# Output projection of three of four token blocks by Strassen's scheme on float32 head sums, and another order of VectorE's work in the first pair of each ConvFFN half

## The chip, the cores and the metric

One NeuronCore of a Trainium2 chip runs the whole kernel. The metric is the device time of one execution in microseconds (us), lower is better. TensorE (PE in the profile) multiplies matrices, VectorE (DVE), ScalarE (ACT) and GpSimd (POOL) work on elements, and SyncE (SP) issues most DMA transfers, in the order of its program.

## The reference

One decoder layer on x of 2048 tokens x 1024, in float32:

```python
h = rms_norm(x, norm_mix_pre)
p = h @ w_in                        # 1024 x 3088: u, v_a, q, k, v_b, g_out, lr
out_a = sgu_mixer(gelu(u), gelu(v_a), ...)       # causal gating in chunks of 128, 4 heads
out_b = rms_norm(gla_mixer(q, k, v_b, gk), ...) * silu(g_out)   # gated linear attention, 4 heads
mix = concatenate([out_a, out_b]) @ w_out        # 1024 x 1024
x = x + rms_norm(mix, norm_mix_post)
h = rms_norm(x, norm_ffn_pre)
up = causal_dwconv(h @ w_up, conv_w, conv_b)     # 1024 x 5632
ff = (gelu(up[..., :2816]) * up[..., 2816:]) @ w_down
x = x + rms_norm(ff, norm_ffn_post)
```

## The kernel before

**Products.** A float32 product is made of three matmuls on float32r operands. ScalarE copies an operand to its rounded high part, and VectorE or GpSimd subtracts that from the operand to get the low part ("split"). The matmuls are high x high, high x low and low x high.

**Mix phase.** Four blocks b0 to b3 of 512 tokens. Each block runs its in-projection, then two things interleaved by `weave`: "main", the linear attention (`gla_half`, matmuls named lv, o, s), and "side", a list of steps. The side of block b is: the rest of the projections g1 and g, the *output projection of block b-1* (`mix_out`), the residual of that block (`x1_steps`: read the mix rows x0m, x1m, ... and the rows of x, write x1), then `va`, `u` and the spatial gating. In block 3 the side also loads x1 rows (`h_load`), transposes and combines them for the ConvFFN (`h_combos`, tiles h0x, h1b, h01s, ...) and stores the seven sums of Strassen's scheme (`act`). Blocks overlap: block 2's first loads (b2xT0 to 3, x transposed) are issued during block 1's last steps.

**Weights.** `weight` gives a piece of two 128 x 512 tiles. At its first use a piece is read raw, copied, split (by GpSimd and VectorE in turn), and both parts are written to DRAM under a key; later blocks read the two parts. The pool has three slots for the parts and two for raw pieces, so the piece three places on can only be read when TensorE has used this one. In `mix_out` a piece (`mx0w0`, ...) serves 24 matmuls: four token tiles, two k-tiles, three matmuls. There are eight pieces, 192 matmuls in a block. Four 128 x 1024 buffers with the tag `xin` hold b2xT, the rows of x1_steps and the tiles of h_load and h_combos.

**Order.** The instruction order of the mix phase comes from a scheduler that works through the code by priority; each engine and each queue then keeps its order. The mix rows are written from ScalarE's queue.

**ConvFFN.** Two halves of 22 pairs, by Strassen's scheme with seven products (`product(m)`) of 12 matmuls each. Beside the products of one pair (`u10` is half 1, pair 0) VectorE adds partial results from PSUM (u2, u3, c22), makes the four sums of the next pair's weights (`sums`, `last_sum`), and does the convolution and the gate of the previous pair; GpSimd splits. In the first pair of a half it also splits operands of the half's activations (`acts`, tiles tal and tbl). Then follows the down projection (d0A, ...).

Of the kernel before, what the change touches and what calls it, by code (L numbers as in the profile page):

```python
# [7 lines left out]
F32 = mybir.dt.float32  # L8
# [9 lines left out]
P = 128  # L18
D = 1024
# [18 lines left out]
def layer_kernel(ctx, tc, x, xT, w_ch, w_gl, w_tk, w_o, w_up, w_dn, w_gk, wsT, cols, conv, rows, sgub,  # L38
# [14 lines left out]
    def scratch(shape, name):  # L53
# [5 lines left out]
    ffs_d = [[[scratch([P, n, T], f"ffs{h}{m}{q}") for q, n in enumerate(GROUPS)] for m in range(7)]  # L59
             for h in range(2)]  # L60
    wdn_d = [[scratch([P, n, T], f"wdn{m}{q}") for q, n in enumerate(GROUPS)] for m in range(7)]

# [58 lines left out]

    def token_steps(srcs, kper, n, hh, hl, name, done, key=None):
        nk = kper * len(srcs)
        ps = [bank(f"{name}a{t}", acc=True) for t in range(TT)]
        for i, src in enumerate(srcs):
            hi, lo = weight(src, kper * n, f"{name}w{i}", key and (key, i))
# [30 lines left out]
    def mix_phase(mp, late):  # L157
# [57 lines left out]
        def mix_in(b, prev):  # L215
# [119 lines left out]

            oh = [late.tile([P, T], F32R, tag="ohi", name=f"{n}oh{h}", bufs=4) for h in range(NH)]
            ol = [late.tile([P, T], F32R, tag="olo", name=f"{n}ol{h}", bufs=4) for h in range(NH)]
            ohb = late.tile([P, NH, T], F32R, tag="ohb", name=f"{n}ohb", bufs=1)
            olb = late.tile([P, NH, T], F32R, tag="olb", name=f"{n}olb", bufs=1)

# [4 lines left out]

            def side():
                def gate(t, ps):
# [3 lines left out]
                yield from token_steps([w_tk[0, i] for i in range(4)], 2, 512, hh, hl, f"{n}g", gate, "g")  # L351
                def g4(nm):
                    return w1.tile([P, D], F32, tag="xin", name=nm, bufs=4)

                if prev is not None:
                    for k, ins in enumerate(mix_out(b - 1, *prev)):
                        if b == 3 and k % 2 == 0:
                            xs = h_load(0, k // 2, g4)
                        yield
                        if b == 3 and k % 2:  # L360
                            with tc.issue_after(ins):
                                h_combos(0, k // 2, xs, g4, g4,
                                         lambda nm: [bank(f"{nm}{k}") for k in range(2)])
                            yield
                    if b < 3:
                        yield from x1_steps(b - 1, gpost, lambda nm: w1.tile([P, D], F32, tag="xin", name=nm, bufs=4))

                va = [w1.tile([P, 512], F32, tag="va", name=f"{n}va{t}", bufs=4) for t in range(TT)]
# [13 lines left out]
                for h in range(NH):  # L382
# [7 lines left out]
                    for t in range(TT):  # L390
# [7 lines left out]
                                           op0=ALU.mult, op1=ALU.add)  # L398
                    V.tensor_tensor(out=z, in0=z, in1=u, op=ALU.mult)
                    A.copy(out=oh[h], in_=z)  # L400
                    split_lo(V, ol[h], z, oh[h])
                    yield
# [10 lines left out]

            weave(main(), side(), (0.8, 0.8) if prev is not None else (0.62, 0.5))
            return oh + [ohb[:, h, :] for h in range(NH)], ol + [olb[:, h, :] for h in range(NH)]

        def mix_out(b, oh, ol):
            n = f"b{b}"
            for half in range(2):
                def evac(t, ps):  # L420
                    m = late.tile([P, 512], F32, tag="mo", name=f"{n}mo{t}", bufs=2)
                    A.copy(out=m, in_=ps)
                    A.activation(out=ps, in_=ps, func=AF.Square, accum_out=ssm[:, b, half, t:t + 1])
                    nc.scalar.dma_start(out=mix_d[b][t * P:(t + 1) * P, half * 512:(half + 1) * 512],
                                        in_=m)
# [11 lines left out]
    def gla_half(b, hb, cum, qT, kT, vb, sg, ohb, olb, state, attn, klow, qup, lvl_sb, sel_sb, w1, pend):  # L437
# [221 lines left out]
    def ffn_phase(fp, mix_rest, late):  # L659
# [266 lines left out]

        def rest_of(f):
            V.tensor_tensor(out=f.g[:, T:], in0=f.g[:, T:], in1=f.u2, op=ALU.add)
            f.conv_first("g")
            f.conv_rest("v")  # L930
            f.keep_halo("v")

        raws = load_up(1)
        for at, (half, j) in enumerate(steps + [(2, 0)]):
# [6 lines left out]
            turn = half == 0 and j == NPAIR - 1  # L941
            new = half == 1 and j == 0
            if at + 1 < len(steps):
                s23, s14 = unit("s", f"{n}s23", 2), unit("s", f"{n}s14", 2)
# [21 lines left out]
            if prev:  # L966
                rest_of(prev)
            if not end:
                f.u2 = w2.tile([P, T], F32, tag="u2", name=f"{n}u2")
                u3 = w2.tile([P, T], F32, tag="u3", name=f"{n}u3")  # L970
                copy_u2 = A.copy(out=f.u2, in_=pa)
            if new:
                op_split(acts[1])
            if nxt:
                nxt.sums()
                nxt.split(0)
            if new:
                op_split(acts[3], G)
            if prev:
# [8 lines left out]
            if prev:  # L988
                prev.conv_rest("g")
                A.activation(out=prev.y, in_=prev.y, func=AF.Gelu_apprx_tanh)  # L990
            product(6, None if end else pc, apart=() if end else (add_u2,))
            if new:
                op_split(acts[2])
            if not end:
                add_u3 = V.tensor_tensor(out=u3, in0=pc, in1=f.u2, op=ALU.add)
            side.turn(0)
            if nxt:
                nxt.last_sum()
                nxt.split(4)
            if prev:  # L1000
                V.tensor_tensor(out=prev.y, in0=prev.y, in1=prev.yv, op=ALU.mult)
                ff.append(prev.y)
# [3 lines left out]
            if nxt:  # L1006
                nxt.split(1)
            if len(ff) == 2:
                ph, pj = steps[at - 1]
                q, i = divmod(pj // 2, 4)  # L1010
                for m, src in stage_sums(f"f{ph}{pj}", *ff):
                    nc.sync.dma_start(out=ffs_d[ph][m][q][:, i, :], in_=src)
                ff = []
            side.sums()
            product(1, None if end else pa, True, () if end else (add_c22,))
            if nxt:
                nxt.split(3)
            if at == 0:
                op_split(acts[2])
            side.turn(1)  # L1020
# [9 lines left out]
            if not end:  # L1030
                V.tensor_tensor(out=pc, in0=pc, in1=f.u2, op=ALU.add)
                f.conv_first("v")
            side.late_sums()
            if turn:
# [120 lines left out]
        for s, (m, half, g) in enumerate(dsteps):  # L1155
# [5 lines left out]
            if s <= last:  # L1161
# [5 lines left out]
                if half == 1 and s + 3 < len(dsteps):  # L1167
                    d_load_w(dsteps[s + 3][0], g)
            if s + 1 < len(dsteps):
                op_split(dt[s + 1])  # L1170
# [109 lines left out]
```

## Time and profile before

| | |
|---|---|
| median of 3 runs | 2161.97 us (2161.17 to 2163.98) |
| profiled execution | 2162.19 us, span 2160.4 us |
| TensorE / VectorE busy | 2081.2 us (96%) / 1456.4 us (67%) |
| ScalarE / GpSimd busy | 885.4 us (41%) / 628.3 us (29%) |
| moved by DMA | 411.46 MB, mean 190 GB/s |

The span is the profiled execution from its first to its last instruction. The shares are means over stages that differ: the mix phase ends at about 842 us, half 0 of the ConvFFN at 1274, half 1 at 1733.

### The profile page before, as it was taken

Reading aid. Unit: us, or ns where it says so; the run is one execution under the profiler, and the core shown is the slowest. Engines: PE = TensorE matmul, PEld = TensorE weight load, DVE = VectorE, ACT = ScalarE, POOL = GpSimd, SP = SyncE. Lnnn points to the kernel's source line nnn. Section 1 sums busy time; section 2 is a strip of 40 time slices with the busy share of each in tenths; the row PEclk is TensorE's granted clock in tenths of the full one; section 3 lists DMA queues with packets and bytes.
Section 4 is the critical chain, followed back from the end, with each engine's and each line's share of the span. In section 5 each row is a group of like instructions: output and inputs, shape, how many; then the busy total and the mean of one; then the engine's idle time right before and its main releaser. Section 6 shows DMA issues by size and latency. Waiting matters only on the chain.

```text
span 2160.4 us, 27160 instructions
## 1 busy us (share of the span) xinstructions
PE 2081.2 (96%) x9904; PEld 1718.5 (80%) x9904; DVE 1456.4 (67%) x2010; ACT 885.4 (41%) x1462; POOL 628.3 (29%) x449
## 2 busy tenths in 40 slices
PE   7999999999999998999999988999999999999998
PEld 6888888887887776888888866887778778888886
DVE  5875646544564434888788789999999952443467
ACT  5444434333345424444555453433333333323252
POOL 2320311111110021555554555555555300000000
PEclk9999999999999999999999998999999999999999
DMA  7884567456656757455355453444444544444467
GB/s 268 284 307 176 168 245 274 156 175 238 232 172 216 257 182 276 150 185 190 108 185 181 132 209 132 161 152 146 150 156 171 196 149 138 145 160 147 142 243 263
DMA packets 160390, 411.46 MB, mean 190 GB/s; under 512 B 15344, under 2 KB 44416, under 8 KB 160256
## 3 DMA queue, kind: packets, MB, share of 16 engines
q1 hardware_dynamic: 155360, 401.22, 54.1%
q10 hardware_dynamic: 4896, 8.50, 1.0%
q8 instruction: 78, 1.28, 0.2%
q14 instruction: 56, 0.46, 0.1%
HBM read 288.42 MB, written 129.89 MB: 194 GB/s over the span
## 4 chain that ended last, share of the span: by engine, by line
PE 42%; DVE 14%; issue 3%; DMA 1%; ACT 1%; DVEq 0%; SPq 0%; POOLq 0%; POOL 0%; ACTq 0%
PE d0D L1119 3%; PE d1C L1119 3%; PE d0C L1119 3%; PE d1A L1119 3%; PE d1D L1119 2%; PE d0A L1119 2%; PE d1B L1119 1%; PE d0B L1119 1%; DMA dw<-in_w_dn 1%; DVE dw L611 1%; DVE ds L612 1%; DVE dw L613 1%; PE u017G L756 1%; PE u015G L756 1%; PE u013G L756 1%
## 5 line engine op out<-in xcount | busy, mean ns | idle before, releaser
L1099 POOL TENSOR_TENSOR o01r<-o01r,mhalf 128x4 f32<-128x4 f32 x1 | 1.0, 1007 | 357.2 <-DVE o01r L1098 357.2
L77 DVE TENSOR_TENSOR tal<-tal,tah 128x1024 fp32r<-128x1024 f32 x14 | 19.8, 1422 | 25.4 <-ACT tah L689 25.4
L494 DVE COPY_PREDICATED attn<-lvl_sb,b3h1lv 128x512 f32<-128x512 uint8 x7 | 6.3, 895 | 26.2 <-PE b3h1lv L491 26.2
L474 POOL TENSOR_TENSOR qup<-b1q,b1h0e 64x256 f32<-64x256 f32 x7 | 9.8, 1406 | 41.9 <-issue 25.1
L689 ACT CAST tah<-tal 128x1024 fp32r<-128x1024 f32 x14 | 14.5, 1047 | 17.2 <-DMA tal<-act 17.2
L474 POOL TENSOR_TENSOR qup<-b2q,b2h0e 64x256 f32<-64x256 f32 x7 | 9.8, 1407 | 40.1 <-issue 23.3
L1119 PE MATMUL d0A<-d0wh,d00th 128*128 128x512 f32 x44 | 17.9, 406 | 2.8 <-DVE u121y L783 2.8
L77 DVE TENSOR_TENSOR d05tl<-d05tl,d05th 128x1024 fp32r<-128x1024 f32 (+1 forms) x6 | 6.6, 1134 | 20.5 <-ACT d05th L689 20.5
L474 POOL TENSOR_TENSOR qup<-b3q,b3h0e 64x256 f32<-64x256 f32 x7 | 8.1, 1156 | 42.0 <-issue 23.4
L77 DVE TENSOR_TENSOR d01tl<-d01tl,d01th 128x1024 fp32r<-128x1024 f32 (+1 forms) x6 | 6.6, 1134 | 20.0 <-ACT d01th L689 20.0
L77 DVE TENSOR_TENSOR d11tl<-d11tl,d11th 128x1024 fp32r<-128x1024 f32 (+1 forms) x6 | 6.5, 1133 | 19.7 <-ACT d11th L689 19.7
L1075 DVE TENSOR_TENSOR r<-d0C,du 128x512 f32<-128x512 f32 x8 | 5.2, 686 | 21.3 <-PE d0C L1119 21.3
L77 DVE TENSOR_TENSOR tbl<-tbl,tbh 128x1024 fp32r<-128x1024 f32 x10 | 13.1, 1353 | 9.3 <-ACT tbh L689 9.3
L1119 PE MATMUL d0A<-d0wl,d00th 128*128 128x512 f32 x44 | 17.8, 404 | 1.2 <-DVE d0wl L77 1.2
L474 POOL TENSOR_TENSOR qup<-b2q,b2h1e 64x256 f32<-64x256 f32 x7 | 5.6, 804 | 44.7 <-PE b2h1lv L491 26.9
L613 DVE TENSOR_TENSOR dw<-dw,ds 128x512 f32<-128x512 f32 x11 | 17.4, 1580 | 0.4
L1119 PE MATMUL d0A<-d0wh,d00tl 128*128 128x512 f32 x44 | 17.6, 400 | 0.0
L611 DVE TENSOR_TENSOR dw<-dw 128x512 f32<-128x512 f32 x11 | 17.4, 1578 | 0.4
L612 DVE TENSOR_TENSOR ds<-dw,dw 128x512 f32<-128x512 f32 x11 | 17.4, 1578 | 0.4
L474 POOL TENSOR_TENSOR qup<-b3q,b3h1e 64x256 f32<-64x256 f32 x7 | 5.7, 817 | 40.7 <-PE b3h1lv L491 35.3
L1119 PE MATMUL d1A<-d0wh,d10th 128*128 128x512 f32 x44 | 17.1, 389 | 0.0
L1119 PE MATMUL d1A<-d0wl,d10th 128*128 128x512 f32 x44 | 17.1, 389 | 0.0
(4495 smaller groups left out, 8168.9 us busy)
## 6 DMA issues: line engine op xcount, KB each, us to landing
dw<-in_w_dn SPq DMA_DIRECT2D x22, 512.0 KB, 5.1
tal<-act SPq DMA_DIRECT2D x14, 512.0 KB, 7.6
tbl<-act SPq DMA_DIRECT2D x14, 512.0 KB, 5.8
wdn<-in_w_dn SPq DMA_DIRECT2D x6, 1024.0 KB, 9.2
out<-r SPq DMA_DIRECT2D x12, 512.0 KB, 8.0
wdn<-dw SPq DMA_DIRECT2D x22, 256.0 KB, 2.4
wdn<-ds SPq DMA_DIRECT2D x22, 256.0 KB, 3.2
d00tl<-ffs SPq DMA_DIRECT2D x5, 512.0 KB, 8.4
```

What stands on the lines that cost most here:

```text
L77: eng.tensor_tensor(out=lo, in0=full, in1=hi.bitcast(F32), op=ALU.subtract)
L474: (G if par else V).tensor_tensor(out=qu[r, :, par, :].rearrange("p a (g s) -> p a g s", s=s), in0=view(q)[r, :, :, 1, :], in1=ev[r, :, :, ...
L494: V.copy_predicated(out=av[:, :, :, 1, :], mask=mk.unsqueeze(1).to_broadcast([P, 8, gc, s]), data=ps.rearrange("p (x g s) -> p x g s", x=8 ...
L611: eng.tensor_tensor(out=b12, in0=b12, in1=b11, op=ALU.subtract)
L612: eng.tensor_tensor(out=t2, in0=b22, in1=b12, op=ALU.subtract)
L613: eng.tensor_tensor(out=t4, in0=b21, in1=t2, op=ALU.subtract)
L689: A.copy(out=hi[:, sl], in_=raw[:, sl])
L756: ins = PE.matmul(ps, lhsT=a[:, sl], rhs=b[:, i], start=not more and i == 0 and k == 0, stop=i == 3 and k == 2, skip_group_check=more)
L1075: return V.tensor_tensor(out=row(half, o[0], t)[:, o[1] * T:(o[1] + 1) * T], in0=ps, in1=u, op=ALU.add)
L1099: G.tensor_tensor(out=rs, in0=rs, in1=mhalf[:, :4], op=ALU.pow)
L1119: ins = PE.matmul(ps, lhsT=lhs, rhs=wop[w][:, i], start=start and k == 0, stop=stop and k == 2, skip_group_check=more)
```

## The change

**The projection.** For blocks 0 to 2 `mix_out_sums` takes the place of `mix_out`. The heads' outputs are kept in float32 (`ar`, `br`), not split. Seven products of Strassen's scheme follow, in the order 0, 1, 5, 6, 3, 4, 2, each on a sum of heads (`operand`) and a sum of weights, with 24 matmuls: 168 in place of 192. There are 14 weight pieces (`mx00`, `mx01`, `mx10`, ...) with 12 matmuls each. s1, s2 and s4 take buffers of the tag xin. The mix rows are written from SP's queue.

**The weight sums.** At the end of block 0's side `mix_sums` reads w_o in 16 loads of 256 KB, makes four sums in each of four steps on VectorE, and writes them in 16 stores.

**Block 3.** Its side calls h_load and h_combos at fixed steps (k = 1, 3, 5, 12, 14, 16). Its own projection stays `mix_out`; in the second half two of its four pieces have no kept parts (their keys are None), since no block before has used them alone.

**First pairs** (`fresh`). VectorE adds PSUM sums first, then the previous pair's convolution, then the weight sums. One operand of half 1 (`acts[3]`) is split by VectorE in place of GpSimd.

```diff
+        def mix_sums(g4):
+            for kt in range(4):
...
+                r1, r2, t = g4(f"ws{kt}a"), g4(f"ws{kt}b"), g4(f"ws{kt}t")
+                for k in range(2):
+                    for r, at in ((r1, i), (r2, 2 + i)):
+                        nc.sync.dma_start(out=r[:, k * T:(k + 1) * T], in_=w_o[k, at][:, sl])
+                ts = combos(V, r1[:, :T], r1[:, T:], r2[:, :T], r2[:, T:], t[:, :T], t[:, T:], r2[:, :T])
+                for m in range(3, 7):
+                    nc.sync.dma_start(out=wmx_d[m][:, kt * T:(kt + 1) * T], in_=ts[m])
+                yield
+
+        def mix_out_sums(b, ar, br, g4):
...
+            s1, s2, s4 = [g4(f"{n}s{k}").rearrange("p (k t) -> p k t", k=NH) for k in (1, 2, 4)]
+            V.tensor_tensor(out=s1, in0=a21, in1=a22, op=ALU.add)
+            V.tensor_tensor(out=a21, in0=a11, in1=a21, op=ALU.subtract)
+            V.tensor_tensor(out=s2, in0=s1, in1=a11, op=ALU.subtract)
+            V.tensor_tensor(out=s4, in0=a12, in1=s2, op=ALU.subtract)
+            src = {0: a11, 1: a12, 2: s4, 3: a22, 4: s1, 5: s2, 6: a21}
+
+            def operand(m):
+                hi, lo = [late.tile([P, NH, H], F32R, tag=f"r{k}", name=f"{n}m{m}{k}", bufs=2) for k in ("hi", "lo")]
+                A.copy(out=hi, in_=src[m])
+                split_lo(V, lo, src[m], hi)
+                return hi, lo
+
+            def keep(t, r, half, x, spare):
+                tt = r * 2 + t
+                A.activation(out=spare, in_=x, func=AF.Square, accum_out=ssm[:, b, half, tt:tt + 1])
+                nc.sync.dma_start(out=mix_d[b][tt * P:(tt + 1) * P, half * T:(half + 1) * T], in_=x)
...
+            for at, m in enumerate(DORDER):
...
+                for i in range(2):
+                    piece = wmx_d[m][:, i * D:(i + 1) * D] if m > 2 else w_o[m // 2, 2 * (m > 0) + i]
+                    wh, wl = weight(piece, D, f"{n}mx{m}{i}", ("mx", m, i))
...
+                keys = [("mx", 0, 0), ("mx", 0, 1), ("mx", 1, 0), ("mx", 1, 1)] if half == 0 else \
+                    [None, None, ("mx", 2, 0), ("mx", 2, 1)]
```

```diff
             if nxt:
-                nxt.sums()
+                if not fresh:
+                    nxt.sums()
                 nxt.split(0)
-            if new:
-                op_split(acts[3], G)
...
                 add_c22 = V.tensor_tensor(out=pb, in0=pd, in1=u3, op=ALU.add)
-            if nxt:
+            if new:
+                op_split(acts[3])
+            if fresh:
+                nxt.sums()
+                nxt.split(5)
+                nxt.split(6)
+                if prev:
+                    conv_g(prev)
+            elif nxt:
                 nxt.split(1)
```

SP's queue in block 1, behind the output projection of block 0. The names: x0m, x1m, x2m, x3m read mix rows, x0x to x3x rows of x, x10 to x13 are the x1 rows written; h and l before 1vaw, 1u, 2g0w and 2qk are the high and low parts of weights. Before, around the first b2xT:

```order
L597 DMA x2x_2961<-in_x 128x1024
L91 DMA hb1u0_3160<-kb0u00_1387 128x1024
L91 DMA lb1u0_3161<-kb0u01_1388 128x1024
L602 DMA x12_71<-x2x_2961 128x1024
L91 DMA hb1u1_3202<-kb0u10_1462 128x1024
L91 DMA lb1u1_3203<-kb0u11_1463 128x1024
L595 DMA x3m_2980<-mix0_85 128x1024
L597 DMA x3x_2982<-in_x 128x1024
L91 DMA hb1u2_3244<-kb0u20_1544 128x1024
L91 DMA lb1u2_3245<-kb0u21_1545 128x1024
L222 DMA b2xT0_3334<-in_xT 128x1024
```

And with the change:

```order
L705 DMA x2x_3061<-in_x 128x1024
L703 DMA x3m_3093<-mix0_85 128x1024
L92 DMA hb2g0w1_3539<-kb1g0w10_1825 128x1056
L92 DMA lb2g0w1_3540<-kb1g0w11_1826 128x1056
L710 DMA x12_71<-x2x_3061 128x1024
L92 DMA hb2qk0_3594<-kb0qk00_412 128x1024
L92 DMA lb2qk0_3595<-kb0qk01_413 128x1024
L705 DMA x3x_3095<-in_x 128x1024
L225 DMA b2xT0_3437<-in_xT 128x1024
L225 DMA b2xT1_3448<-in_xT 128x1024
```

The first read of block 2's input has moved from behind the third `u` piece to behind the first `qk` piece of block 2, and the residual's chain with it.

SP's queue with the change in block 3, where block 2 is projected and the second group of h rows is stored (act, from the tiles h1b, h1x, h5x and h01s of h_combos; mx50 is the first weight piece of product 5):

```order
L92 DMA hb2mx50_6035<-kb0mx500_2611 128x1024
L92 DMA lb2mx50_6036<-kb0mx501_2612 128x1024
L753 DMA act04_93<-h1x_5717 512x1x128
L753 DMA act05_94<-h5x_5720 512x1x128
L92 DMA hb2mx51_6051<-kb0mx510_2633 128x1024
L92 DMA lb2mx51_6052<-kb0mx511_2634 128x1024
L92 DMA hb2mx60_6093<-kb0mx600_2681 128x1024
L92 DMA lb2mx60_6094<-kb0mx601_2682 128x1024
L753 DMA act03_92<-h01s_5852 512x1x128
L753 DMA act06_95<-h5x_5720 512x1x128
```

The last store out of h5x, whose buffer is used again for s2, now stands behind three weight pieces of the projection.

VectorE in the first pair of half 1 before (u10s14 and u10s23 are weight sums of the next pair, u10u2 and u10u3 the additions from PSUM, tbl the low parts of the half's activations):

```order
L77 TENSOR_TENSOR tbl1_10679<-tbl1_10679,tbh1_10678 128x1024 x2
L708 TENSOR_TENSOR u10s14_10742<-u1rv_10556 128x512
L709 TENSOR_TENSOR u10s23_10741<-u1rg_10555,u1rv_10556 128x512
L710 TENSOR_TENSOR u10s23_10741<-u10s14_10742,u1rg_10555 128x512
L984 TENSOR_TENSOR u10u2_10767<-u10V_10748,u10u2_10767 128x512
L780 SCALAR_TENSOR_TENSOR u021y_10762<-u021G_10559,cv_6762,u021y_10762 128x1023
L780 SCALAR_TENSOR_TENSOR u021y_10762<-u021G_10559,cv_6762,u021y_10762 128x1022
L77 TENSOR_TENSOR tbl2_10738<-tbl2_10738,tbh2_10737 128x1024 x2
L995 TENSOR_TENSOR u10u3_10768<-u10V_10748,u10u2_10767 128x512
```

And with the change:

```order
L1109 TENSOR_TENSOR u10u2_10933<-u10V_10917,u10u2_10933 128x512
L1117 TENSOR_TENSOR u10u3_10934<-u10V_10917,u10u2_10933 128x512
L78 TENSOR_TENSOR tbl1_10848<-tbl1_10848,tbh1_10847 128x1024 x2
L888 SCALAR_TENSOR_TENSOR u021yv_10884<-u021V_10729,cv_6927,u021yv_10884 128x1023
L888 SCALAR_TENSOR_TENSOR u021yv_10884<-u021V_10729,cv_6927,u021yv_10884 128x1022
L1129 TENSOR_TENSOR u10V_10917<-u10G_10916,u10u3_10934 128x512
L78 TENSOR_TENSOR tbl3_10876<-tbl3_10876,tbh3_10875 128x1024 x2
L816 TENSOR_TENSOR u10s14_10911<-u1rv_10725 128x512
L817 TENSOR_TENSOR u10s23_10910<-u1rg_10724,u1rv_10725 128x512
L818 TENSOR_TENSOR u10s23_10910<-u10s14_10911,u1rg_10724 128x512
```

Both additions now stand ahead of the weight sums and of two splits, and the split of tbl3 is new on this engine.

## Rows read from the trace of the kernel before

**Rows 1.** The page: its head, and part 1, busy time of each engine.

```profile
span 2160.4 us, 27160 instructions
PE 2081.2 (96%) x9904; PEld 1718.5 (80%) x9904; DVE 1456.4 (67%) x2010; ACT 885.4 (41%) x1462; POOL 628.3 (29%) x449
```

**Rows 2.** Stretches of the span; the first line names the columns.

```profile
core 0: us, PE busy (x) PEld busy (x) DVE busy (x) ACT busy (x) POOL busy (x), PEclk, DMA share, GB/s
100.00:150.00 50.00, 48.80 (x267) 41.05 (x267) 36.19 (x74) 22.16 (x34) 15.01 (x13) 1.00 0.93 319
150.00:200.00 50.00, 48.93 (x287) 41.56 (x286) 31.30 (x62) 22.20 (x45) 5.44 (x4) 1.00 0.62 219
...
1330.00:1700.00 370.00, 364.80 (x1584) 295.74 (x1583) 355.82 (x415) 144.09 (x206) 199.23 (x130) 1.00 0.45 154
...
257.00:312.40 55.40, 55.19 (x284) 45.47 (x282) 22.90 (x50) 25.42 (x54) 12.84 (x10) 1.00 0.67 236
455.00:509.90 54.90, 54.90 (x283) 45.48 (x282) 17.20 (x47) 16.89 (x46) 5.57 (x7) 1.00 0.53 183
```

**Rows 3.** TensorE's timeline near 308 and 370: start, duration, instruction.

```profile
307.65 0.39 PE L135 MATMUL b0mx1a<-hb0mx1w,b0olb 128*128 128x512 f32 x1
...
310.43 0.39 PE L135 MATMUL b0mx1a<-hb0mx1w,b0olb 128*128 128x512 f32 x1
...
369.60 0.39 PE L120 MATMUL b1u<-b1hi,lb1u 128*128 128x512 f32 x1
...
370.63 0.37 PE L133 MATMUL b2g0a<-hb2g0w,b2hi 128*128 128x264 f32 x1
```

**Rows 4.** DMA from 255 to 372 in 40 slices; issues, KB, median us to landing.

```profile
GB/s 259 275 129 382 153 232 179 144 410 300 403 351 95 277 78 280 6 244 297 189 391 413 115 307 231 297 385 286 304 332 394 346 214 304 338 250 309 185 185 133
...
rb0mx1w<-in_w_o SPq DMA_DIRECT2D x4, 512.0 KB, 4.8
...
lb1vaw<-kb0vaw SPq DMA_DIRECT2D x4, 512.0 KB, 5.0
...
b2xT<-in_xT SPq DMA_DIRECT2D x4, 512.0 KB, 6.5
```

**Rows 5.** SP's queue from 300 to 352: start, issue time, transfer.

```profile
310.25 0.32 SPq L595 DMA_DIRECT2D x0m<-mix  x1
...
344.66 0.38 SPq L222 DMA_DIRECT2D b2xT<-in_xT  x1
```

**Rows 6.** Groups by line, 255 to 313: busy, mean ns; idle time before.

```profile
L95 ACT CAST hb0mx1w<-rb0mx1w 128x1024 fp32r<-128x1024 f32 x4 | 4.2, 1049 | 6.6 <-PE b0mx0a L135 6.6
...
L77 DVE TENSOR_TENSOR lb0mx1w<-rb0mx1w,hb0mx1w 128x1024 fp32r<-128x1024 f32 x2 | 2.5, 1230 | 6.3 <-ACT hb0mx1w L95 6.3
...
L77 POOL TENSOR_TENSOR lb0mx1w<-rb0mx1w,hb0mx1w 128x1024 fp32r<-128x1024 f32 x2 | 4.8, 2398 | 12.1 <-DMA mix<-b0mo 10.2 <-ACT hb0mx1w L95 1.9
```

**Rows 7.** DMA issues from 685 to 706, columns as in rows 4.

```profile
act<-h5x SPq DMA_DIRECT2D x2, 256.0 KB, 4.7
```

**Rows 8.** TensorE's waits in the whole span: total, times, longest, in us.

```profile
PE u10V L756 <- DVE u10u L995: 13.8, 1, 13.8
...
PE b3mx0a L133 <- DMA hb3mx0w<-kb0mx0w: 3.8, 1, 3.8
...
PE u00V L756 <- DVE u00u L995: 2.2, 1, 2.2
```

**Rows 9.** Stretches behind two waits of TensorE, columns as in rows 2.

```profile
200.59:204.00 3.41, 3.41 (x9) 2.65 (x9) 0.60 (x1) 3.38 (x3) 0.00 (x0) 0.50 0.00 0
...
791.10:797.90 6.80, 5.89 (x15) 4.11 (x14) 0.00 (x0) 0.62 (x1) 0.41 (x1) 0.50 0.92 370
```

**Rows 10.** VectorE's timeline in the first pair of half 1.

```profile
1290.20 2.82 DVE L709 TENSOR_TENSOR u10s<-u1rg,u1rv 128x512 f32<-128x512 f32 x1
...
1300.99 2.36 DVE L77 TENSOR_TENSOR tbl<-tbl,tbh 128x1024 fp32r<-128x1024 f32 x2 [2.12 <-ACT tbh L689]
...
1308.86 0.68 DVE L796 TENSOR_TENSOR f021b<-u020y 128x512 f32<-128x512 f32 x1
```

More of the change, by code (lines that the diff above doesn't have):

```diff
@@ L60, in layer_kernel @@
              for h in range(2)]
+    wmx_d = {m: scratch([P, 4 * T], f"wmx{m}") for m in range(3, 7)}
     wdn_d = [[scratch([P, n, T], f"wdn{m}{q}") for q, n in enumerate(GROUPS)] for m in range(7)]
@@ L120, in chan_mm, with token_steps @@
             PE.matmul(ps, lhsT=lo[:, sl], rhs=hh[kt], start=False, stop=(kt == KT - 1))
-    def token_steps(srcs, kper, n, hh, hl, name, done, key=None):
+    def token_steps(srcs, kper, n, hh, hl, name, done, keys=None):
+        if isinstance(keys, str):
+            keys = [(keys, i) for i in range(len(srcs))]
         nk = kper * len(srcs)
@@ L344, in mix_in, with g4, steps @@
                 sgu_consts()
-            def side():
+            def g4(nm):
+                return w1.tile([P, D], F32, tag="xin", name=nm, bufs=4)
+            def steps():
                 def gate(t, ps):
@@ L351, in side @@
                 yield from token_steps([w_tk[0, i] for i in range(4)], 2, 512, hh, hl, f"{n}g", gate, "g")
-                def g4(nm):
-                    return w1.tile([P, D], F32, tag="xin", name=nm, bufs=4)
                 if prev is not None:
[L356 to L364, printed above, removed]
+                    yield from mix_out_sums(b - 1, *prev, g4)
                     if b < 3:
-                        yield from x1_steps(b - 1, gpost, lambda nm: w1.tile([P, D], F32, tag="xin", name=nm, bufs=4))
+                        yield from x1_steps(b - 1, gpost, g4)
                 va = [w1.tile([P, 512], F32, tag="va", name=f"{n}va{t}", bufs=4) for t in range(TT)]
@@ L398, in side @@
                                            op0=ALU.mult, op1=ALU.add)
-                    V.tensor_tensor(out=z, in0=z, in1=u, op=ALU.mult)
-                    A.copy(out=oh[h], in_=z)
-                    split_lo(V, ol[h], z, oh[h])
+                    if whole:
+                        V.tensor_tensor(out=z, in0=z, in1=u, op=ALU.mult)
+                        if h % 2 == 0:
+                            o2, l2 = [late.tile([P, 2, T], F32R, tag=f"r{k}", name=f"{n}o{k}{h}", bufs=2)
+                                      for k in ("hi", "lo")]
+                        oh.append(o2[:, h % 2])
+                        ol.append(l2[:, h % 2])
+                        A.copy(out=oh[h], in_=z)
+                        split_lo(V, ol[h], z, oh[h])
+                    else:
+                        V.tensor_tensor(out=ar[:, h], in0=z, in1=u, op=ALU.mult)
+                    yield
+                if b == 0:
+                    yield from mix_sums(g4)
+            def side():
+                if b < NB - 1:
+                    yield from steps()
+                    return
+                xs = None
+                for k, _ in enumerate(steps()):
+                    if k in (3, 5, 14, 16):
+                        with tc.issue_after(newest_pe()):
+                            h_combos(0, (3, 5, 14, 16).index(k), xs, g4, g4,
+                                     lambda nm: [bank(f"{nm}{i}") for i in range(2)])
+                    if k in (1, 3, 12, 14):
+                        xs = h_load(0, (1, 3, 12, 14).index(k), g4)
                     yield
@@ L942, in ffn_phase @@
             new = half == 1 and j == 0
+            fresh = new or at == 0
             if at + 1 < len(steps):
@@ L1005, in ffn_phase @@
                 add_c22 = V.tensor_tensor(out=pb, in0=pd, in1=u3, op=ALU.add)
-            if nxt:
-                nxt.split(1)
[L1008 to L1013, printed above, removed]
+            if new:
+                op_split(acts[3])
[4 more added lines that the diff above has]
+                if prev:
+                    conv_g(prev)
+            elif nxt:
+                nxt.split(1)
+            if end:
+                op_split(dt[1])
+                op_split(dw[DORDER[0], 1])
+            if len(ff) == 2 and not fresh:
+                stage()
             side.sums()
             product(1, None if end else pa, True, () if end else (add_c22,))
+            if fresh:
+                op_split(acts[2])
+                nxt.last_sum()
+                nxt.split(4)
+                nxt.split(1)
+                if prev:
+                    close_y(prev)
             if nxt:
                 nxt.split(3)
-            if at == 0:
-                op_split(acts[2])
             side.turn(1)
```

107 lines of the change are left out of this document (87 added, 20 removed).

## The prediction

> **What bounds the kernel now.** I read the page first, then stretches of it, then single waits. TensorE is busy 2081.2 of 2160.4 us [rows 1], so whatever ends sooner must first make TensorE's list shorter or its waits fewer. But the page is an average, and two stretches are bound otherwise. In half 1 of the ConvFFN, VectorE is busy 355.82 of 370 us beside TensorE's 364.80: both at once [rows 2]. And in the mix phase the transfers are near what they ever reach: the highest 50 us, at 100 to 150, move 319 GB/s with the DMA engines busy for 0.93 of the time [rows 2]. The reader should keep these two in mind, since the change takes matmuls from the mix phase and adds transfers to it.
>
> The projection of block 0 is bound by TensorE before: from its first matmul to the first of `b1va` 55.40 us pass, 55.19 of them busy [rows 2]. Matmuls of 128x512 follow each other every 0.2315 us: twelve take from 307.65 to 310.43 [rows 3].
>
> **The change part by part.**
>
> *Fewer matmuls.* Seven products of 24 matmuls in place of 192: 24 less per block, 72 in all, times 0.2315 = **-16.7 us**. This is what can be gained in the mix phase, and the form of the matmul (128x512) does not change.
>
> *Block 0's own projection (in block 1).* Here each weight piece is used for the first time: it is read raw (524 KB), and its high and low parts are written out to be kept (1049 KB), so 1.573 MB per piece. Before, eight pieces come at 24 matmuls each; now fourteen at 12 each. In bytes: 14 x 1.573 = 22.0 MB and 2.1 MB of mix rows, against 12.6 + 2.1. TensorE needs 55.4 - 24 x 0.2315 = 49.8 us, with GLA's matmuls that lie between. About 1.6 MB (three raw pieces) is read ahead, and the kept parts of the last three pieces (3.1 MB) follow after, so 19.4 MB must pass in 49.8 us: 390 GB/s. The nearest row with the same traffic is 100 to 150, at 319 GB/s: 60.8 us, **+11**. Bounds: 0, since single slices of 2.9 us reach 413 GB/s [rows 4]; +16, since with two raw buffers a piece needs its landing of 4.8 us [rows 4], a copy of 1.05 and a split of 1.23 or 2.40 (VectorE and GpSimd in turn, mean 1.8) [rows 6], so 7.65 / 2 = 3.8 us against TensorE's 49.8 / 14 = 3.56: +4 from that alone, and both limits can hit different pieces.
>
> By the Trainium skill ("DMA: Bandwidth & Descriptors", Specifications) the fabric's ceiling is 435 GB/s. By it 19.4 MB would take an estimated 45 us and this term would be 0; the slice of 413 speaks for that, no row of 50 us does.
>
> *What comes behind the projection on SP's queue.* The order shows x0m, x1m, ... (the reads of the mix rows for the residual) moved behind `va` and `u` weights. Before, x0m is issued at 310.25, ahead of block 1's `va`, and the first b2xT at 344.66, right behind the third `u` piece [rows 5]. Now hb2qk0 stands ahead of b2xT0. It is the third piece after u3, and the weight pool has three slots, so it is issued only when TensorE has used u3. Before, the last matmul on u3 starts at 369.60 and b2g0a at 370.63 [rows 3]: b2xT had landed long ago. Now it is issued at about 370.0 plus four issues of 0.35, lands 6.5 later [rows 4], and ScalarE and VectorE make the operand in about 1.2 more (half of a copy and a split of twice the size [rows 6]): 379.1 against 370.63, **+8.5**. Bounds +5 (a landing of 3) and +14 (x3x, which stands ahead too, waits for its slot first). At the next block the same chain has its kept weights and a shorter queue: **+1** (0 to +6).
>
> *Head sums.* In blocks 0 to 2 the operands are made as seven copies and splits of 1.05 and 1.23 [rows 6]; VectorE has 49.8 us for 7 x 1.23, four sums and eight additions of about 0.7, about 20 us in all, beside 22.9 us of its own [rows 2]: hidden, save in block 3. There s1, s2, s4 take the slots (tag xin) that h_combos leaves. s2 gets that of h5x, whose last store (act06) stands on SP behind hb2mx60 and lb2mx60. These are the seventh piece, issued when the fourth is used, which is the end of the second product; the third product needs s2. So TensorE waits: four issues (about 2), the store's landing 4.7 [rows 7], the sum (1.23), the copy 1.05 and part of the split [rows 6]; 9 less what the order of banks gives back: **+8.5** (bounds 0, if the slots fall otherwise, and +11).
>
> *Weight sums in block 0.* 16 loads and 16 writes of 256 KB (8.4 MB) and 16 sums of 128x512. Half of it falls into 100 to 150, the fullest stretch: 4.2 MB less the 1.2 MB that a share of 0.93 leaves free, at 343 GB/s = 9 us at most; the other half falls into the next 50 us, at a share of 0.62 [rows 2]. **+6** (0 to +12).
>
> *Block 3's own projection* now has two of its pieces raw. 4.8 + 1.05 + 2.4 = 8.3 us is less than the 11.1 us of two pieces ahead, but TensorE waits there already, 3.8 for the first kept piece [rows 8]: **+2** (0 to +8).
>
> *First pairs.* In half 0 TensorE waits 2.2 for an addition that stands behind weight sums [rows 8]; it now stands ahead: **-2** (0 to -4). In half 1 it waits 13.8 for the same addition [rows 8], which now comes before the sums. But all of half 1 is bound by VectorE too [rows 2], so what counts is when VectorE is done: a sum takes 2.82 there, while GpSimd splits, and 0.68 elsewhere [rows 10]; two or three of them give about -5.4; the split that VectorE takes over costs 2.36 [rows 10]; a wait of 2.12 for ScalarE may shrink: **-4** (0 to -8).
>
> *Clock.* After a wait of some us TensorE runs at 0.50 for 3.4 us, or twice that (6.8 us after the wait at b3mx0a) [rows 9]: the granted clock is then 1.2 GHz, and half of that time is lost. Four or five new waits (block 0's pieces, b2g0a, block 3) cost 4 x 1.7: **+7** (+3 to +10).
>
> Sum: -16.7 + 11 + 8.5 + 1 + 8.5 + 6 + 2 - 2 - 4 + 7 = **+21.3**. The profiled execution took 2162.19 us, 0.2 above the median of 2161.97, so the forecast is **2183** (its own range 2173 to 2196).
>
> **The rivals.**
> 1. *Everything added is hidden* (faster). The transfers keep 390 GB/s or more in block 0, and the slots in block 3 fall well: 2162 - 16.7 - 2 - 4 + about 2 = 2141. It decides at one weight piece of 1.573 MB per 3.56 us. For it: slices of 413 GB/s. Against it: no 50 us above 319, and the two waits on SP's order (8.5 each) need no bandwidth to occur. With one of them it is 2150. Chance 0.12.
> 2. *The projection of block 0 keeps pace, the two waits remain.* 2183 - 11 - 3 (two stretches of half clock) = 2169; with the weight sums hidden too, 2163, no change. The rate of 435 would do this. Chance 0.22 in all, 0.07 of it within 0.2%.
> 3. *The kept loads stall as well.* In blocks 1 and 2 a piece is 1.049 MB per 3.56 us, 295 GB/s, and 337 with the mix rows; before, this stretch has 183 GB/s [rows 2]. By 319 the three slots just cover it. If not, up to +8 in each: 2199. Against it: a kept part lands in 5.0 us [rows 4], with two pieces (7.1 us) ahead. Chance 0.16.
>
> **How the numbers follow.** The forecast has 0.50. A measurement can tell 0.2% here, 4.3 us. Faster is rival 1: 0.12; same 0.07; slower the rest, 0.81. The range reaches from the middle between rivals 1 and 2, 2156, to 2204, where rival 3 ends with its clock.
>
> **What would show it.** In block 1, TensorE's waits on the weights named mx, the stretch of the projection longer than 55.4 us although it has 24 matmuls less, and a DMA share above 0.9. At b2g0a, a wait of about 8 on b2hi. In block 3, a wait ahead of the third product on b2m5. In half 1 the wait of 13.8 gone, but the start of the second pair earlier by 4 only. The forecast is wrong if pieces land in step with 3.56 us, or if SP's order does not hold x3m and b2xT back.

## The result

With the change the kernel takes **2203.08 us** (median of 6 runs, 2200.44 to 2205.24), before 2162.7 beside it: ratio 1.0187, 95% interval [1.0174, 1.0199]. It is 40 us slower. The forecast was 2183 in a range of 2156 to 2204: the right sign, but half the size. The range holds the result with 0.9 us to spare.

The page of the kernel with the change, its head and part 1, against [rows 1]:

```profile
span 2203.1 us, 27206 instructions
PE 2082.6 (95%) x9832; PEld 1718.1 (78%) x9832; DVE 1519.0 (69%) x2071; ACT 900.5 (41%) x1467; POOL 634.1 (29%) x451
```

TensorE has 72 matmuls less and is busy 1.4 us *longer*. That is the first thing to explain. The mix phase as one stretch shows it, first before, then after (columns as in rows 2; one fence for each kernel):

```profile
0.00:842.10 842.10, 802.68 (x4308) 671.54 (x4308) 461.31 (x902) 347.58 (x654) 153.35 (x133) 0.99 0.66 227
```

```profile
0.00:887.60 887.60, 800.60 (x4236) 670.43 (x4236) 523.72 (x961) 363.29 (x659) 164.34 (x137) 0.96 0.72 248
...
100.00:150.00 50.00, 47.46 (x264) 39.97 (x262) 35.24 (x72) 23.05 (x37) 16.07 (x14) 1.00 0.88 311
150.00:200.00 50.00, 46.34 (x256) 40.52 (x255) 32.78 (x58) 19.83 (x38) 4.87 (x3) 0.90 0.86 293
...
268.50:337.90 69.40, 56.95 (x259) 45.11 (x258) 39.77 (x68) 34.32 (x63) 22.83 (x13) 0.88 0.83 292
495.80:551.70 55.90, 54.84 (x300) 45.23 (x299) 32.42 (x67) 18.77 (x41) 7.26 (x7) 1.00 0.85 296
```

From 842.1 to 887.6 the mix phase grew by 45.5 us. The matmuls left out are worth 16.7, but busy time fell by only 2.1: the other 14.6 went into matmuls at the lower clock (mean 0.96, before 0.99). By the traces' record of the clock there are twelve stretches at 0.50 up to u00V with the change, and five before. TensorE's (PE) busy time in them, summed, with the change and then before:

```profile
sum 78.51, PE 56.16 PEld 48.17 DVE 44.82 ACT 28.72 POOL 14.11; mean PE 4.68 PEld 4.01 DVE 3.73 ACT 2.39 POOL 1.18
```

```profile
sum 23.89, PE 20.82 PEld 16.42 DVE 7.49 ACT 15.02 POOL 0.44; mean PE 4.16 PEld 3.28 DVE 1.50 ACT 3.00 POOL 0.09
```

At 0.50 up to half of that busy time is lost: 28.1 and 10.4, a difference of 17.7, which covers the 14.6. Idle time of TensorE rose from 39.4 to 87.0, by 47.6. So 47.6 + 14.6 - 16.7 = 45.5. The projection of block 0 takes 69.4 us, before 55.4 [rows 2].

TensorE's waits name the places, against [rows 8]; those of 3.9 and more:

```profile
PE b0mp L496 <- POOL lb0mx L78: 12.3, 4, 4.6
PE b2mp L494 <- ACT b2m5hi L467: 10.6, 1, 10.6
PE b2g0a L136 <- ACT b2hi L230: 8.9, 1, 8.9
PE b0g0a L136 <- ACT hb0g0w L96: 6.5, 1, 6.5
PE b3mx1a L137 <- POOL lb3mx1w L78: 4.5, 1, 4.5
PE b3mx0a L137 <- DMA lb3mx0w<-kb0mx: 3.9, 1, 3.9
PE b3mx0a L136 <- DMA hb3mx0w<-kb0mx: 3.9, 1, 3.9
```

b0mp is block 0's projection, b2mp block 2's. Of these, before had only b0g0a's and the last one (3.8) at this size; its own largest, 13.8 at u10V [rows 8], is gone. When each stage starts (first matmul on TensorE's timeline; the kernels of the last three columns come below):

| first matmul | before | change | not kept | no weight sums | all moved |
|---|---|---|---|---|---|
| b1g0a, block 1 | 170.8 | 181.2 | 178.8 | 171.6 | 170.2 |
| projection of block 0 | 257.0 | 268.5 | 268.7 | 258.8 | 257.1 |
| b1vaa, behind it | 312.4 | 337.9 | 327.0 | 326.8 | 315.5 |
| b2g0a, block 2 | 370.6 | 404.7 | 386.6 | 394.1 | 376.2 |
| b3g0a, block 3 | 568.7 | 605.8 | 594.8 | 594.7 | 574.7 |
| b3mx0a | 780.9 | 822.4 | 811.2 | 810.8 | 782.3 |
| u00V, ConvFFN | 842.1 | 887.6 | 868.7 | 877.1 | 837.3 |
| u11G | 1312.4 | 1352.3 | 1337.3 | 1344.4 | 1304.7 |
| d0A | 1725.2 | 1769.2 | 1754.9 | 1761.2 | 1721.4 |

### The profile page after: what moved, and what is told of

It is laid out like the page before. It is cut to its first block, busy times and chain, and to the rows that moved or that the text cites. A ratio compares the mean times of both kernels' runs of the same rounds, so it can differ in the third digit from the quotient of the medians.

```text
span 2203.1 us, 27206 instructions
## 1 busy us (share of the span) xinstructions
PE 2082.6 (95%) x9832; PEld 1718.1 (78%) x9832; DVE 1519.0 (69%) x2071; ACT 900.5 (41%) x1467; POOL 634.1 (29%) x451
## 4 chain that ended last, share of the span: by engine, by line
PE 56%; DVE 18%; issue 4%; DMA 3%; ACT 3%; POOL 1%; SPq 0%; DVEq 0%; POOLq 0%; ACTq 0%
PE d0D L1257 3%; PE d1C L1257 3%; PE d0C L1257 3%; PE d1A L1257 3%; PE d0A L1257 3%; PE d1D L1257 3%; PE d1B L1257 1%; PE d0B L1257 1%; DVE ds L720 1%; DVE dw L719 1%; DVE dw L721 1%; PE b2mp L494 1%; PE b2mp L498 1%; PE b2mp L496 1%; PE b1mp L498 1%
## 5 line engine op out<-in xcount | busy, mean ns | idle before, releaser
L96 ACT CAST hb0mx<-rb0mx 128x1024 fp32r<-128x1024 f32 x14 | 14.6, 1044 | 26.9 <-DMA kb0mx<-hb0mx 20.9
L78 POOL TENSOR_TENSOR lb0mx<-rb0mx,hb0mx 128x1024 fp32r<-128x1024 f32 x7 | 18.6, 2664 | 22.1 <-DMA kb0mx<-lb0mx 11.3
L580 POOL TENSOR_TENSOR qup<-b3q,b3h1e 64x256 f32<-64x256 f32 x7 | 6.4, 918 | 56.6 <-PE b3h1lv L597 45.5
L580 POOL TENSOR_TENSOR qup<-b1q,b1h0e 64x256 f32<-64x256 f32 x7 | 7.7, 1108 | 44.2 <-issue 25.7
L136 PE MATMUL b2g0a<-hb2g0w,b2hi 128*128 128x264 f32 x32 | 10.3, 323 | 8.9 <-ACT b2hi L230 8.9
L1257 PE MATMUL d0A<-d0wl,d00th 128*128 128x512 f32 x44 | 17.7, 401 | 0.0
## 6 DMA issues: line engine op xcount, KB each, us to landing
tal<-act SPq DMA_DIRECT2D x14, 512.0 KB, 10.4
```

The lines of the kernel that those rows point to most:

```text
L78: eng.tensor_tensor(out=lo, in0=full, in1=hi.bitcast(F32), op=ALU.subtract)
L96: A.copy(out=hi[:, :n], in_=raw[:, :n])
L580: (G if par else V).tensor_tensor(out=qu[r, :, par, :].rearrange("p a (g s) -> p a g s", s=s), in0=view(q)[r, :, :, 1, :], in1=ev[r, :, :, ...
L1257: ins = PE.matmul(ps, lhsT=lhs, rhs=wop[w][:, i], start=start and k == 0, stop=stop and k == 2, skip_group_check=more)
```

## The experiments

Kernels that ran together share the runs of the kernel before beside them. It took 2164.5 (median of 13) beside e1 to e4, 2168.2 (one run) beside e5 to e8 and 2165.0 (median of 11) beside e9 to e11, with single runs up to 8 us to either side. Only e1 (10 runs) and e9 (6) were run more than once. So of the kernels with one run I read the stages in the trace, and from the time only large differences.

**e1, the ConvFFN part alone**, on the kernel before. This part of the change also moves two splits of the down projection's operands ahead. Its core:

```diff
             if nxt:
-                nxt.sums()
+                if not fresh:
+                    nxt.sums()
                 nxt.split(0)
-            if new:
-                op_split(acts[3], G)
...
+            if fresh:
+                nxt.sums()
+                nxt.split(5)
+                nxt.split(6)
```

> The kernel before with only the ConvFFN part of the change (order in the first pair of each half, the splits moved at the end). By the prediction's step 2 + 4 us are gained: 2156 to 2157. By the theory formed from the trace after, the 4 us at the second pair of half 1 are given back pair by pair, since VectorE sets the pace of half 1 and its work for the later pairs is the same: second pair 4 earlier, last pair level with before, and the time within 2 us of before (2160 to 2163).

Measured: 2160.81 us, ratio 0.9985 [0.9969, 1.0002]: no change that can be told; the interval allows a gain of up to 6.7 us, so the time does not separate the two theories. The trace does: u11G comes at 1306.9, 5.5 earlier than before, and u121G, the last pair's, at 1703.2, 1.5 earlier. The second theory holds. The stretch from the third pair to the last, in this kernel and in the kernel before:

```profile
1327.60:1703.20 375.60, 369.06 (x1597) 298.12 (x1596) 361.43 (x419) 145.79 (x209) 204.67 (x134) 1.00 0.45 154
```

```profile
1331.60:1704.70 373.10, 367.90 (x1597) 298.30 (x1596) 358.96 (x418) 145.87 (x209) 202.30 (x132) 1.00 0.45 155
```

The same 1597 matmuls take 2.5 us longer when they begin earlier. VectorE is busy 96.2% of both, so 2.5 us longer as well: one instruction more of its list falls into the stretch (419, before 418).

**e2, the projection part alone** (the ConvFFN as before).

> The change without its ConvFFN part. If the two parts do not touch each other, the first matmul of the ConvFFN stands 45 us later than before, as with the whole change, and the time is 2203 to 2206. If the ConvFFN part cost something of its own in the whole change, it is below 2200.

Measured: 2207.25, 1 us above what was expected, u00V at 886.3 (44.2 later than before) and d0A 45.1 later. The whole loss is the projection's, and the ConvFFN part gives back 1 to 2 of it.

**e3, nothing kept.**

```diff
-wh, wl = weight(piece, D, f"{n}mx{m}{i}", ("mx", m, i))
+wh, wl = weight(piece, D, f"{n}mx{m}{i}")
...
-f"{n}mx{half}", evac, keys)
+f"{n}mx{half}", evac)
```

> The change, but no projection piece has its parts written and kept: each block reads it raw, copies and splits it again (0.52 MB for 1.57 MB in block 1, 0.52 for 1.05 in blocks 2 and 3). Theory kept parts (the writes fill the DMA engines, or hold the weight slots): the waits on the low parts in block 1 (12.3 us) fall below 4, the stretch from the first matmul of the projection to the first of va falls from 69.4 to 54 to 58, b2g0a waits under 3, the time is 2180 to 2188. Rival GpSimd (its splits of 2.7 us are the limit by themselves): waits of 6 or more on GpSimd stay in block 1 and come up in blocks 2 and 3 too, and the time is 2192 or more.

Measured: 2190.43, the projection 58.3 us in place of 69.4, both just above what the theory of kept parts gave. What ScalarE's copy of a raw piece waited for in that stretch, with the change and then in e3 (columns as in rows 6):

```profile
L96 ACT CAST hb0mx<-rb0mx 128x1024 fp32r<-128x1024 f32 x12 | 12.5, 1044 | 24.6 <-DMA kb0mx<-hb0mx 20.9 <-DMA rb0mx<-wmx 3.0 <-PE b1h0o L643 0.6
...
L78 POOL TENSOR_TENSOR lb0mx<-rb0mx,hb0mx 128x1024 fp32r<-128x1024 f32 x6 | 16.2, 2696 | 22.0 <-DMA kb0mx<-lb0mx 11.3 <-ACT hb0mx L96 10.7
```

```profile
L96 ACT CAST hb0mx<-rb0mx 128x1024 fp32r<-128x1024 f32 x12 | 12.5, 1044 | 12.5 <-DMA rb0mx<-wmx 9.1 <-DMA rb0mx<-in_w_o 2.6 <-PE b0mp L498 0.7
```

With the change the copy waits 20.9 us for `kb0mx<-hb0mx`: the *write* of the high part that held this slot before. The raw piece is there; its destination is not free. In e3 that wait is gone. One wait of 2.6 on GpSimd's low part stays (12.3 with the change), as my theory allowed. The writes' bytes are gone too: the stretch moves 166 GB/s, with the change 292.

e3 also settled what holds b2g0a. In its order b2xT0 stands behind hb1u3 again, ahead of both 2g0w pieces and of hb2qk0:

```
L92 DMA lb1u3_3336<-kb0u31_1594 128x1024
...
L225 DMA b2xT0_3381<-in_xT 128x1024
L92 DMA hb2g0w0_3408<-kb1g0w00_1744 128x1056
```

and b2g0a waits 0.4 in all, in place of 8.9.

**e4, the splits of projection pieces all on VectorE, parts kept.**

```diff
-split_lo(G if wcount[0] % 2 and n <= 1024 else V, lo[:, :n], raw[:, :n], hi[:, :n])
+split_lo(G if wcount[0] % 2 and n <= 1024 and "mx" not in name else V, lo[:, :n], raw[:, :n], hi[:, :n])
```

> The change with all splits of projection pieces on VectorE, none on GpSimd; parts kept as in the change. Rival GpSimd: the waits on low parts are gone, the projection takes 55 to 58, the time is near 2190. Theory kept parts: the waits stay under another name (VectorE's low part, or ScalarE's high part), the projection takes 63 or more, the time is 2195 or more.

Measured: 2198.72, the projection 65.2 us. The waits stay under VectorE's name:

```profile
PE b0mp L496 <- DVE lb0mx L78: 7.9, 3, 3.4
```

So the kept parts are the larger cause (11.1 us of the stretch in e3) and GpSimd a smaller one (4.2 here). The 4.2 alone is weak evidence, since e7 takes off 3.7 without touching the splits; e11 supports it (62.4 there, against 58.4 in e9).

**e5, no weight sums** (mix_sums left out; the products that need them read pieces of w_o as they are, so the kernel leaves out a part of the work).

> The change without mix_sums: the weight sums are left out and their products read pieces of w_o as they are, so only the time counts. If the weight sums alone make block 0 longer, the first matmul of block 1 comes at 171 (before 170.8, with the change 181.2), the rest runs as with the change, and the time is 2191 to 2195. If the float32 head sums or the moved loads share in it, 174 or more of these 181 stay.

Measured: 2198.15, in the group where before took 2168.2. b1g0a comes at 171.6, 0.8 behind before, with the change 10.4: the weight sums alone cost 9.6 there. The waits behind it are those of the change. The time is 30 above before, with the change 40.

**e6, as many bytes without holding slots.** Nothing kept, and four writes from the operand tiles per product in block 1.

```diff
+if b == 0:
+    for k in range(2):
+        nc.sync.dma_start(out=scratch([P, D], f"dm{m}{i}{k}"), in_=(hi, lo)[k].rearrange("p k t -> p (k t)").bitcast(F32))
```

> As the kernel whose projection pieces are not kept, but in block 1 four writes of 0.52 MB per product go out from the operand tiles, so that as many bytes are written as with the change, while no weight slot waits for a write. Theory slots (a slot held until its parts are written): the projection's stretch in block 1 stays at 55 to 60 us, with waits below 5. Theory DMA rate: it comes back to 64 or more. What comes behind on SP's queue is pushed back by these writes, so the whole time says nothing.

Inconclusive. The stretch took 60.3 us, just above what the theory of slots says, but only 215 of its 259 matmuls fell into it, and 221 GB/s were moved in it against 292: the writes had slipped behind the projection. Whether the slots or the rate of the transfers weigh more in block 1 stays open. What speaks for the slots is that the DMA share there is 0.83, less than the 0.93 of [rows 2], and that e7 moves more in the same stretch, 307 GB/s.

**e7, the mix rows written from ScalarE's queue.**

```diff
-nc.sync.dma_start(out=mix_d[b][tt * P:(tt + 1) * P, half * T:(half + 1) * T], in_=x)
+nc.scalar.dma_start(out=mix_d[b][tt * P:(tt + 1) * P, half * T:(half + 1) * T], in_=x)
```

> The change with the mix rows written from ScalarE's queue, as before the change. In the order b2xT0 still stands right behind hb2qk0, but x3x and the row writes are not ahead of it. By the prediction's step (b2xT0 can't be issued before TensorE has used u3) the wait at b2g0a stays at 7 to 8.5. Rival (the writes on SP's queue delay it): the wait falls below 3, and the time by 6 or more beyond what the projection itself gains.

Measured: 2201.27. The wait at b2g0a is 6.9, a little under the 7 to 8.5 of the step, and far above the rival's 3: the writes are not what holds b2xT back, its place behind hb2qk0 is. With the change that place reads so on SP, and so on TensorE:

```profile
394.71 0.32 SPq L92 DMA_DIRECT2D hb2qk<-kb0qk  x1
...
396.39 0.82 SPq L225 DMA_DIRECT2D b2xT<-in_xT  x2
```

```profile
394.51 0.39 PE L121 MATMUL b1u<-b1hi,lb1u 128*128 128x512 f32 x1
394.74 1.05 PE L389 MATMUL b1sz<-ws_sb,b1va 128*128 128x128 f32 x8
404.69 0.59 PE L136 MATMUL b2g0a<-hb2g0w,b2hi 128*128 128x264 f32 x1 [8.89 <-ACT b2hi L230]
```

hb2qk is issued 0.2 us after TensorE's last use of u3 begins; b2xT follows it 1.7 later. Before, b2xT was issued 26 us ahead of b2g0a [rows 3, 5].

e7 shows one more thing, for which the prediction has no term: the projection of block 0 takes 65.7 us here, in place of 69.4 (in e2, e5 and e8, which also write the rows from SP's queue, 68.0 to 70.2). So the row writes on SP's queue seem to cost it some us, by one trace.

**e8, the head sums in place.**

```diff
-s1, s2, s4 = [g4(f"{n}s{k}").rearrange("p (k t) -> p k t", k=NH) for k in (1, 2, 4)]
+s1 = g4(f"{n}s1").rearrange("p (k t) -> p k t", k=NH)
...
+if at == 0:
+    V.tensor_tensor(out=a11, in0=s1, in1=a11, op=ALU.subtract)
+    V.tensor_tensor(out=a12, in0=a12, in1=a11, op=ALU.subtract)
```

> The change, but s2 and s4 are written over the heads' sums a11 and a12 once these have been split, so that only s1 takes a buffer of the tag xin. By the prediction's step the wait of 10.6 ahead of the third product in block 3 falls below 2. If nothing else binds there, b3mx0a comes 10 earlier and the time is near 2193. Rival (the chain of h rows sets the pace of block 3's side, and now starts to run into the same place): the gain is given back by b3mx0a or u00V, and the time stays within 4 of the change.

Measured: 2207.78 with before at 2168.2, so the same 40 us. The waits in block 3:

```profile
PE b2mp L495 <- ACT b2m5hi L465: 6.2, 1, 6.2
PE h3t L746 <- ACT h3x L731: 4.7, 1, 4.7
```

The first fell from 10.6 to 6.2 only, and a new one came up at h3t, so that b3mx0a starts 2.3 later than with the change. My step was right about which wait there is, and wrong that removing it pays: the h rows come next on the same side. The rival holds. VectorE's timeline shows how, with the change and then in e8:

```profile
718.20 1.23 DVE L461 TENSOR_TENSOR b2s<-b2s,b2ar 128x1024 f32<-128x1024 f32 x1 [2.04 <-DMA act<-h01s]
```

```profile
708.63 0.69 DVE L722 TENSOR_TENSOR h01s<-h1b,h5x 128x512 f32<-128x512 f32 x1 [1.98 <-DMA act<-h1x]
```

With the change s2 waits for the store of h01s, which is itself made only when a store of h1x has landed (VectorE begins it at 709.80, after a wait of 1.67). In e8 the sums need no buffer, but they stand on VectorE behind h01s, and h01s still waits for h1x.

**e9, all four moved**, as the causes read after e8: not kept, splits on VectorE (as in e3 and e4), and

```diff
-if b == 0:
-    yield from mix_sums(g4)
+ws = mix_sums(g4) if b == 1 else iter(())
+for _ in token_steps([w_tk[0, i] for i in range(4)], 2, 512, hh, hl, f"{n}g", gate, "g"):
+    next(ws, None)
+    yield
...
-if k in (3, 5, 14, 16):
+if k in (1, 3, 13, 15):
...
-if k in (1, 3, 12, 14):
+if k in (0, 1, 11, 13):
```

> The change with its four costs taken away as far as the runs named them: projection pieces not kept, their splits all on VectorE, the weight sums made beside block 1's gate projection instead of at the end of block 0, and the h rows of block 3 loaded and combined earlier (loads at steps 0, 1, 11, 13, combinations at 1, 3, 13, 15). If these are the causes, the 72 matmuls less come through: 2146 to 2158, faster than before and than the change. Rival (splits and copies of raw pieces in each block cost as much as the kept parts did, or the stalls come from the float32 sums themselves): 2165 or more.

Measured: **2148.94 us** (2145.22 to 2158.40), ratio to before **0.9924 [0.9905, 0.9943]**: faster than both kernels, the rival is out. The profiled run was the slowest of the six, 2158.4, so its stages in the table show less than the median gains; where the rest of the gain lies was not traced. Its largest waits and the two stretches:

```profile
PE b0g0a L136 <- ACT hb0g0w L96: 6.5, 1, 6.5
PE b3mx0a L136 <- ACT hb3mx0w L96: 4.9, 1, 4.9
PE b0mp L495 <- ACT b0m6hi L468: 3.9, 1, 3.9
```

```profile
257.10:315.50 58.40, 51.75 (x259) 41.81 (x258) 49.32 (x81) 32.75 (x60) 6.58 (x7) 0.97 0.58 197
0.00:837.30 837.30, 793.58 (x4236) 661.72 (x4237) 558.86 (x1003) 393.34 (x691) 148.83 (x129) 0.98 0.66 224
```

Now busy time of the mix phase is 9.1 below that of before, and idle time 43.7 against 39.4. In the projection VectorE is busy 49.32 of 58.40, nearly as long as TensorE (51.75). Which of the two, or of the loads of raw pieces, sets that stretch next is not shown.

**e10, e9 with the h rows at the steps of the change**, and **e11, e9 with GpSimd and VectorE in turn.**

> The same as the kernel before it in this list, but the h rows stay at the steps of the change. By the theory on s2's buffer a wait of 6 to 10 stands ahead of the third product of block 3 again, and the time is 6 to 11 above that kernel. Rival (this wait is made up later in block 3, as it was with the sums in place): within 3 of it.

Measured: 2156.17. The wait ahead of the third product is back (5.7 us), but u00V starts at 838.5, 1.2 behind e9's profile. In the trace the rival holds, as in e8. The time is 7.2 above e9's median, within what the theory gave, but e9's own runs reach from 2145 to 2158, so a single run says nothing.

Taken away one at a time, the kept parts (e3), GpSimd's splits (e4) and the weight sums (e5) move u00V forward by 18.9, 6.2 and 10.5 us, 35.6 in all; moved together, in e10, by 49.1. The costs do not simply add up, and the single experiments understate them. Why was not tested.

> The first kernel of this list with the splits of projection pieces by GpSimd and VectorE in turn, as in the change. Theory GpSimd (without kept parts its splits are what is left): waits on GpSimd's low parts of 2 to 4 us in blocks 1 and 2 and the time 8 to 18 above the first kernel. Rival (GpSimd is hidden once nothing is kept): within 3 of it.

Measured: 2169.41, 20 above e9's median, where 8 to 18 was expected; in the traces u00V comes 14.6 later. The projection takes 62.4, and its clock is 0.92. Of the expected waits on GpSimd's low parts two showed, in the projections of blocks 1 and 2 (2.6 and 2.2 us); in that of block 0 TensorE waits for operands that VectorE makes late (2.8). So GpSimd's splits cost, partly through VectorE.

## Why the prediction came out as it did

The sign was right and so were most of the mechanisms; the sum of 21.3 was 19 us short. TensorE's idle time by stage, from the traces of both kernels, beside the price of the waits there:

| stage | before | change | more | priced |
|---|---|---|---|---|
| to b1g0a (weight sums) | 14.9 | 21.4 | 6.6 | 6 |
| to the projection of block 0 | 1.1 | 2.8 | 1.7 | 0 |
| projection of block 0 | 0.2 | 12.4 | 12.2 | 11 |
| b1vaa to b2g0a | 2.3 | 10.7 | 8.4 | 8.5 |
| b2g0a to b3g0a | 3.7 | 7.4 | 3.7 | 1 |
| b3g0a to b3mx0a (s2) | 7.5 | 18.6 | 11.1 | 8.5 |
| b3mx0a to u00V | 9.7 | 13.6 | 3.9 | 2 |
| sum | 39.4 | 87.0 | 47.6 | 37 |

So the waits came out 10.6 above their prices and the clock 7.6, and of the 6 us priced as a gain in the ConvFFN 2.8 came (the spans grew by 42.7). Step by step:

- *Fewer matmuls, -16.7.* The count is right. Busy time shows 2.1 of it, see the clock.
- *Block 0's projection, +11.* The idle time of 12.2 comes near, but not by the way that I priced. I had priced bytes at a rate; the sign that I named for that, a DMA share above 0.9, did not come (0.83, at 292 GB/s). TensorE waits 12.3 there on low parts, and these come late because a slot for parts is taken until its write has landed (e3) and because of the splits (e4, e11). My bounds had the slots of raw pieces alone, not the slots of the parts and their writes (and their two terms add up to +15, not +16). So the number is luck. Whether the write's time or its bytes weigh more stays open (e6). The stretch is 14.0 longer than before: 12.2 idle, 7.3 of busy time at a clock of 0.88, less 5.6. By the Trainium skill ("DMA: Bandwidth & Descriptors", Specifications) an estimate with the fabric's 435 GB/s would have made this term 0. The stretch moves 292 at a share of 0.83, so the ceiling was not what bound it.
- *b2g0a, +8.5.* Measured 8.9 as a wait, 8.6 between b1vaa and b2g0a (+25.5 to +34.1). The reasoning from the order was right in each part: the place behind hb2qk0, then issue, landing, copy (e3, e7). *At the next block, +1:* b3g0a waits 2.8.
- *s2's slot, +8.5.* The wait is 10.6, at the place forecast. The slot is another: s2 waits for the store of h01s, not for the last one out of h5x, and that store landed 7.0 us after its issue, where the step had 4.7. Both stores stand behind the same weight pieces on SP's queue. Block 2's projection to b3mx0a grew by 3.4 us, where -5.6 + 8.5 = 2.9 was expected. But e8 and e10 show that the wait is mostly a place where the h rows' chain is paid, not a cause of its own.
- *Weight sums, +6.* Measured 9.6 (e5), within the bounds of 0 to 12. Of the 10.4 by which b1g0a comes later with the change, 6.6 are idle time; the rest is busy time at a mean clock of 0.95, before 0.98.
- *Block 3's own projection, +2.* From b3mx0a to u00V 4.0 were lost.
- *First pair of half 0, -2.* -1.2. *Half 1, -4.* This failed as a step: u11G is 4.4 earlier, d0A 0.3 (after against before, both counted from u10G). The pairs behind have a pace of their own, 19.8 us in place of 19.6 until the last pair (e1). The lead was TensorE's. VectorE is busy 427.6 us from u10G to d0A, before 428.2: its work was moved, not lessened. What sets this pace beside VectorE's 96% I did not separate.
- *Clock, +7.* Measured 14.6 in the mix phase, twice its price. I had counted four or five stretches behind the long waits; there were seven more than before. The chip also went to half clock behind short ones:

```profile
451.13:457.96 6.83, 6.83 (x33) 6.83 (x32) 3.97 (x11) 2.45 (x4) 2.25 (x2) 0.50 0.00 0
```

This follows a wait of 1.96 us (b2h0kps), and all of its 6.83 us are busy, so up to 3.4 are lost. My reading of [rows 9], "after a wait of some us", had missed it: the first stretch there stands behind a wait of only 0.86 us (at 197.74), and the trace of before has two more of 3.41 us, at 688.70 and 736.49, behind waits of 1.82 and 2.20.

Of the rivals, the kept loads of blocks 1 and 2 did not stall: block 1's projection took 55.90 with no wait above 1 us, at 296 GB/s, where I had 295 to 337 as its need. The upper end of the range, 2204, was that rival's time. So it is luck that the range holds the result. Rival 1 was given two conditions that differ: 390 GB/s, and a piece of 1.573 MB per 3.56 us, which is 442 GB/s. Neither was met.

## What to carry to other kernels

A weight that is written back for later use can cost more than a sum of bytes shows: its slot is held until the write has landed, and whatever reads the next piece waits behind it. When fewer matmuls are bought with more and smaller pieces, count each piece's way through the slot (load, copy, split, write) against the matmuls that it now serves, and compare with reading it again; here leaving out the writes took 11 us off a stretch of 69 (how much of it is the slot and how much the bytes stays open). And read the queue's order for what now stands behind a load that waits for a slot: that is where the rows of the next block were found. And take costs away together before you judge a change: one at a time they gave 13 us at most here, together 54.

## What was not expected of the hardware

A wait of 1.96 us was followed by 6.83 us at a granted clock of 0.50 (1.2 GHz), as long as behind the wait of 3.8 us before [rows 9]. Another stretch of 6.83 us, from 150.76, begins within the second of two waits close together, of 2.54 and 1.10 us.

The three weight sums of the first pair of half 1 take 0.69 each on VectorE when GpSimd does not split beside them, and took up to 2.82 when it did [rows 10]. The Trainium skill ("SBUF — State Buffer", Who interferes with whom) says that a VectorE instruction with two inputs in SBUF contends with a GpSimd instruction that reads SBUF. The rows agree; this is the second sum with the change, while GpSimd is idle, where [rows 10] has 2.82 beside a split:

```profile
1340.23 0.69 DVE L817 TENSOR_TENSOR u10s<-u1rg,u1rv 128x512 f32<-128x512 f32 x1
```
